# SwiGLU's input projection as seven products of quarters instead of eight, with the sums on GpSimd

## The chip, the cores and the metric

The kernel runs on one core of one Trainium2 chip. The metric is the device time of one execution in microseconds (us); lower is better. Of a kernel that is compared, several runs are made and the median is given.

The engines are TensorE (PE, matmuls; PEld is its weight load), VectorE (DVE), ScalarE (ACT), GpSimd (POOL) and SyncE (SP, which here issues the loads). Each has a queue of its own that is worked off in order; the Tile framework puts the instructions into the queues and adds semaphores.

## The reference

A trunk of two layers over 512 tokens of width 1024. Each layer has a mixer (a causal convolution group beside gated linear attention, with one output projection), a cross-attention into 256 memory tokens, and a SwiGLU block, each with a residual and a layer norm. What the change touches is the first product of SwiGLU:

```python
def swiglu(x, w_in, w_out):
    g, u = jnp.split(x @ w_in, 2, axis=-1)
    return (jax.nn.silu(g) * u) @ w_out

    # in the layer
    h = layer_norm(DEEPNORM_ALPHA * h + xa, ln2_g[l], ln2_b[l])
    ff = swiglu(h, w_ffn_in[l], w_ffn_out[l])
```

`w_in` is 1024 x 5632, the two halves of its columns being g and u (2816 each); `w_out` is 2816 x 1024. All is float32.

## The kernel before

**Products in three passes.** TensorE multiplies in a shorter float format (fp32r). Each operand is therefore split into a high part (`hi`, a copy by ACT that rounds) and a low part (`lo = src - hi`, a subtraction by DVE, or by POOL for some weights): `split`, L93 to L95. A product is three matmuls, hi·hi, hi·lo and lo·hi (`mm3`, L129 to L132), summed in a bank of PSUM. There are eight banks: four with the tag acc, two tr, two cv.

**Weights.** A chunk of 512 KB (128 partitions x 1024) is loaded by SP into one of three `stage` buffers (`raw`), split by ACT and DVE into a buffer of `ring` (four) and used (`wchunk`, L114). Which engine does the low part is set by `wlo_engines`; from the cross-attention on it is DVE for all.

**Layer norm.** `out_proj` (L244) adds the residual for each tile of 128 tokens (`tt`) and calls `layer_norm` (L168): statistics on DVE, a chain of small DVE operations for 1/sqrt (`rstd_of`), two passes over the tile with scale and bias (L177 and L183), then eight transposes on PE into two banks (`lt_ln`, L191), each bank copied to hi by ACT and to lo by DVE (L194). The transposed result hT is the moving operand of the next product, 512 tokens wide.

**SwiGLU** (L697 to L727). The 2816 columns are done in pairs of 256 columns (j = 0, 2, ... 20: eleven pairs a layer). For each pair the product has g's 256 columns and u's 256 columns: four chunks of weights, in four banks, 96 matmuls of 512 tokens. The pair j = 0 is done in two halves of 256 tokens, so that it can begin before the last tiles of the layer norm are there. Then ACT takes silu of g from PSUM, DVE multiplies by u from PSUM (L712), and the product is split into ph and pl. The pairs come in three parts (four, four and three pairs), and behind each part an output projection (`out_proj`, `po_fo`) adds its share to h. The first part's first pair stands right behind the layer norm called LN2.

**Order.** The framework's scheduler places the instructions; operations under `tc.high_priority` (the evacuation of the banks, the norms) go ahead of others. Buffers are taken from pools, and a transfer or an operation that fills a buffer waits for the last reader of what was in it.

Of the kernel before, what the change touches and what calls it, by code (L numbers as in the profile page):

```python
# [20 lines left out]
P = 128  # L21
# [18 lines left out]
RING = 4  # L40
HP = 1500
# [6 lines left out]
def trunk(ctx: ExitStack, tc, a, out):  # L48
# [26 lines left out]
    # keep s <= c in both 64-blocks [s, c]  # L75
# [10 lines left out]
    attT = const.tile([P, 2, 4, P], F32, name="attT")  # L86
    DVE.memset(attT, 0.0)
# [4 lines left out]
    # ------------------------------------------------------------ helpers  # L92
# [21 lines left out]
    def wchunk(src, nk, ncol, name, resident=False):  # L114
        """src: dram [nk*128, ncol] -> (hi, lo) views [128, nk, ncol]."""
# [52 lines left out]
    def layer_norm(tt, st, gb, name, hT=None, store=None):  # L168
# [11 lines left out]
        for i in range(2):  # L180
# [11 lines left out]
            pv = pt.rearrange("p (k t) -> p k t", k=4)  # L192
            ts_ = slice(tt * P, (tt + 1) * P)
# [50 lines left out]
    def out_proj(w, stat, name, scale, norm=None, fin=False):  # L244
        """h[tt] = scale*h[tt] + stat^T w, t-tile after t-tile; stat: list of (hi, lo) [128, T]."""
# [25 lines left out]
    # ------------------------------------------------------------ memory of the cross-attention  # L271
# [31 lines left out]
    # ------------------------------------------------------------ input norm  # L303
# [50 lines left out]
    for l in range(L):  # L354
        n_ = lambda s: f"{s}_{l}"
        w_in = a["w_in"][l]
        # -------------------------------------------------- per-layer constants
# [35 lines left out]
        def conv_taps(half):  # L393
            cts = range(half * 2, half * 2 + 2)
            cv = {ct: bank(n_(f"cv{ct}"), tag="cv") for ct in cts}
            with tc.high_priority(offset=-100000):
# [7 lines left out]
                for ct in cts:  # L404
                    ACT.activation(acc[:, ct, :], cv[ct], AF.Copy)
# [71 lines left out]
        # -------------------------------------------------- GLA state updates  # L477
# [25 lines left out]
        # -------------------------------------------------- conv norm and activation  # L503
# [3 lines left out]
        def conv_norm():  # L507
            for g in range(2):
# [4 lines left out]
                for i in range(2):  # L513
# [3 lines left out]
                    for ct in range(4):  # L517
                        PE.transpose(pt[:, ct * P:(ct + 1) * P], acc[:, ct, tt * P:(tt + 1) * P], ident)
# [6 lines left out]
                for i in range(2):  # L525
                    tt = g * 2 + i
                    ACT.activation(acc[:, :, tt * P:(tt + 1) * P], pts[i].rearrange("p (c f) -> p c f", c=4),
                                   AF.Identity, scale=y2[:, i:i + 1], bias=b2[:, i:i + 1])
# [220 lines left out]
```

## Time and profile before

| | us |
|---|---|
| runs: median (lowest to highest) | 1457.99 (1457.73 to 1458.32) |
| the profiled execution's span | 1456.5 |
| PE busy | 1427.5 (98%) |
| DVE busy | 843.2 (58%) |
| ACT busy | 489.4 (34%) |
| POOL busy | 180.5 (12%) |

The span is that of the one execution that the profiler took, the runs are timed from outside: the median lies 1.5 us above it. The profile's page gives busy times, 40 slices of the span and the chain of work that ended last. The trace behind it is asked in views: groups of instructions of one form (with busy time, mean ns of one and the idle time before them), the timeline (start in us, length in us, engine, line, operation, output<-inputs, and how many in a row are put together), and windows (the busy time of each engine in a stretch). Where instructions of one kind stand back to back, a length read from the timeline of several is shorter than the mean of one, since their ends overlap.

### The profile page before, as it was taken

The numbers are of one execution on the slowest core, as the hardware profiler recorded it, in microseconds if no ns is written. First come the engines' busy times: TensorE is split into PE (matmuls) and PEld (weight loads), VectorE is DVE, ScalarE is ACT, GpSimd is POOL, SyncE is SP. The second block draws the span as 40 slices with busy tenths as digits, with TensorE's granted clock in tenths as the row PEclk, the third lists the DMA queues.
The fourth block names the chain that finished last, engine by engine and source line by source line (L and its number), as shares of the span: only waits on it lengthen the run. The fifth ranks groups of instructions, "written<-read, shape, count | busy, mean of one in ns | idle before, by whom it ended". The sixth has DMA issues, their size and how long they took to land.

```text
span 1456.5 us, 18479 instructions
## 1 busy us (share of the span) xinstructions
PE 1427.5 (98%) x7503; PEld 1209.9 (83%) x7503; DVE 843.2 (58%) x1423; ACT 489.4 (34%) x720; POOL 180.5 (12%) x82
## 2 busy tenths in 40 slices
PE   8999999999999999999989999999999999999997
PEld 7777878988988888888888878899889888888886
DVE  6699878557433233333769996675583333342347
ACT  5553452441322123123235335324423222330330
POOL 3576220000000000000143422200000000000000
PEclk9999999999999999999999999999999999999999
DMA  6424241221333232232252323512312332331431
GB/s 230 139 73 131 86 175 59 88 76 48 123 101 116 73 101 91 83 116 94 68 156 79 100 76 129 175 59 88 116 57 90 101 101 87 101 111 49 131 116 58
DMA packets 102953, 147.43 MB, mean 101 GB/s; under 512 B 6844, under 2 KB 81296, under 8 KB 102868
## 3 DMA queue, kind: packets, MB, share of 16 engines
q1 hardware_dynamic: 102548, 145.98, 30.7%
q8 instruction: 59, 0.97, 0.3%
q10 hardware_dynamic: 320, 0.27, 0.1%
q14 instruction: 26, 0.21, 0.0%
HBM read 144.13 MB, written 2.10 MB: 100 GB/s over the span
## 4 chain that ended last, share of the span: by engine, by line
PE 81%; DVE 15%; ACT 2%; issue 1%; DMA 0%; POOL 0%; SPq 0%; DVEq 0%; ACTq 0%; POOLq 0%
PE pp_f L130 11%; PE pp_f L132 11%; PE pp_f L131 11%; DVE cv L403 8%; PE po_fo L130 5%; PE po_fo L132 5%; PE po_fo L131 5%; PE pp_xq L131 2%; PE pp_xq L130 2%; PE pp_xq L132 2%; PE po_mo L130 2%; PE po_mo L132 2%; PE po_xo L132 2%; PE po_mo L131 2%; PE po_xo L130 2%; PE po_xo L131 2%
## 5 line engine op out<-in xcount | busy, mean ns | idle before, releaser
L131 PE MATMUL pp_f<-hT_ln,w_f 128*128 128x512 f32 (+1 forms) x768 | 285.1, 372 | 0.0
L130 PE MATMUL pp_f<-hT_ln,w_f 128*128 128x512 f32 (+1 forms) x768 | 284.4, 372 | 0.0
L132 PE MATMUL pp_f<-hT_ln,w_f 128*128 128x512 f32 (+1 forms) x768 | 283.8, 371 | 0.0
L95 DVE TENSOR_TENSOR w_f<-raw_f,w_f 128x1024 fp32r<-128x1024 f32 x88 | 106.8, 1225 | 196.4 <-ACT w_f L94 196.4
L94 ACT ACTIVATE w_f<-raw_f 128x1024 fp32r<-128x1024 f32 x88 | 91.9, 1057 | 282.0 <-PE po_fo L132 125.9
L131 PEld LDWEIGHTS pp_f<-hT_ln,w_f 128*128 128x128 f32 x768 | 144.7, 188 | 24.9
L132 PEld LDWEIGHTS pp_f<-hT_ln,w_f 128*128 128x128 f32 x768 | 144.5, 188 | 25.0
L130 PEld LDWEIGHTS pp_f<-hT_ln,w_f 128*128 128x128 f32 x768 | 144.2, 188 | 24.9
L403 DVE SCALAR_TENSOR_TENSOR cv<-u,chan,cv 128x511 f32<-128x511 f32 (+28 forms) x240 | 158.8, 732 | 0.3
L131 PE MATMUL po_fo<-w_fo,ph 128*128 128x512 f32 (+1 forms) x358 | 138.2, 386 | 0.0
L132 PE MATMUL po_fo<-w_fo,pl 128*128 128x512 f32 (+1 forms) x358 | 137.8, 385 | 0.0
L130 PE MATMUL po_fo<-w_fo,ph 128*128 128x512 f32 (+1 forms) x358 | 135.7, 385 | 0.0
L95 POOL TENSOR_TENSOR w_c<-raw_c,w_c 128x1024 fp32r<-128x1024 f32 x16 | 39.1, 2458 | 552.4 <-ACT w_c L94 552.4
L263 DVE SCALAR_TENSOR_TENSOR h<-h,po_fo 128x512 f32<-128x512 f32 (+1 forms) x49 | 32.8, 675 | 118.0 <-PE po_fo L132 117.5
L95 DVE TENSOR_TENSOR w_fo<-raw_fo,w_fo 128x1024 fp32r<-128x1024 f32 x44 | 53.0, 1222 | 82.5 <-ACT w_fo L94 82.5
L94 ACT ACTIVATE hT_ln<-lt_ln 128x512 fp32r<-128x512 f32 x40 | 22.7, 596 | 169.7 <-PE lt_ln L191 169.4
L130 PEld LDWEIGHTS po_fo<-w_fo,ph 128*128 128x128 f32 x358 | 67.2, 188 | 13.5
L131 PEld LDWEIGHTS po_fo<-w_fo,ph 128*128 128x128 f32 x358 | 67.2, 188 | 13.4
L132 PEld LDWEIGHTS po_fo<-w_fo,pl 128*128 128x128 f32 x358 | 67.3, 188 | 13.4
L94 ACT ACTIVATE w_fo<-raw_fo 128x1024 fp32r<-128x1024 f32 x44 | 45.4, 1054 | 61.0 <-PE pp_f L132 23.0
L131 PE MATMUL pp_xq<-hT_ln,w_xq 128*128 128x256 f32 (+1 forms) x192 | 61.2, 321 | 0.0
L132 PE MATMUL pp_xq<-hT_ln,w_xq 128*128 128x256 f32 (+1 forms) x192 | 60.7, 319 | 0.0
(252 smaller groups left out, 2840.8 us busy)
## 6 DMA issues: line engine op xcount, KB each, us to landing
raw_f<-w_ffn_in SPq DMA_DIRECT2D x88, 512.0 KB
raw_fo<-w_ffn_out SPq DMA_DIRECT2D x44, 512.0 KB
raw_xk<-w_xkv SPq DMA_DIRECT2D x16, 512.0 KB
raw_c<-w_in SPq DMA_DIRECT2D x16, 512.0 KB
raw_xv<-w_xkv SPq DMA_DIRECT2D x16, 512.0 KB
raw_mo<-w_mix_out SPq DMA_DIRECT2D x16, 512.0 KB
raw_xq<-w_xq SPq DMA_DIRECT2D x16, 512.0 KB
raw_xo<-w_xo SPq DMA_DIRECT2D x16, 512.0 KB
```

Of the source, the lines that this page charges most:

```text
L94: ACT.activation(hi, src, AF.Copy)
L95: eng.tensor_sub(lo, src, f(hi))
L130: PE.matmul(o, lh, rh, start=start, stop=False)
L131: PE.matmul(o, lh, rl, start=False, stop=False)
L132: PE.matmul(o, ll, rh, start=False, stop=stop)
L263: DVE.scalar_tensor_tensor(h[tt][:, c0:c1], h[tt][:, c0:c1], scale, bks[c][:, :c1 - c0], ALU.mult, ALU.add)
L403: DVE.scalar_tensor_tensor(cv[ct][:, s:], u[:, ct, :T - s], wj, cv[ct][:, s:], ALU.mult, ALU.add)
```

## The change

Let g's and u's columns of a pair (256 of each) and the 1024 rows of the weight be cut so that the weight is 2 x 2 quarters: r11 and r12 are g's columns with the upper and lower 512 rows, r21 and r22 are u's. The activations are cut in the same way: rows of 512 and tokens of 256. A product of 2 x 2 quarters takes eight products of quarters, or seven with sums before and after them (one level of Strassen's method, in Winograd's form). For the pairs j = 2 to 20 the change takes the seven.

- **Sums of activations, once a layer.** The class `Quads` takes the place of hT for LN2. Besides hi and lo (`B`), ACT copies each transposed bank as it is to `qr`, and POOL forms four differences of 128x512 from these for each of the last two tiles (L301 to L304). `combine` splits the four results into T2, T3, T1, T4.
- **Sums of weights, for each pair.** POOL forms s1 = r21 + r22 (L360), s2 = s1 - r11 (L361), s3 = r11 - r21 (L364) and s4 = r12 - s2 (L368), each 128x1024. Seven buffers are split instead of four.
- **Seven products** of 2 x 4 x 3 = 24 matmuls of 256 tokens each, in the order P1, P6, P2, P7, P5, P4, P3. P1 and P2 sum in banks X (acc), P7 and P4 in W (acc), P6 stands in Y (cv), P5 and P3 in Z (cv).
- **Sums of results.** ACT copies X's first product to x. DVE adds u2 = Y + x (L400), uu = W + u2 (L411), + Z (L416), uu's other half = W + u2 (L420) and sg = Z + u2 (L425), each twice with 128x256 out of PSUM; ACT takes silu of both halves, DVE multiplies (L427) and the result is split.
- **j = 0** stays eight products (`swiglu_plain`).
- **Pools.** `stage` has five buffers instead of three, `tmp` four instead of three, `blk` fifteen instead of seventeen; new are `evp` (five) and `quad` (three of 128x1024, which hold s1 to s4, and in the mixer the convolution's acc in two halves and attT, which POOL now clears). With acc in halves, L527's operation of 512 columns becomes two of 256. At the start of the kernel the x tiles 2 and 3 are loaded one 512 KB chunk of weights later than before.

```diff
+        def take(self, i, tt, pv):
+            s = slice((tt % 2) * P, (tt % 2 + 1) * P)
+            b = self.b[i, tt // 2]
+            split(b[:, 0, :, s], b[:, 1, :, s], pv)
+            ACT.activation(self.raw[tt // 2][:, i, :, s], pv, AF.Copy)
+            if i == 1 and tt >= 2:
+                r11, r21 = (self.raw[0][:, x, :, s] for x in range(2))
+                r12, r22 = (self.raw[1][:, x, :, s] for x in range(2))
+                POOL.tensor_sub(r11, r12, r11)
+                POOL.tensor_sub(r12, r22, r12)
+                POOL.tensor_sub(r22, r22, r11)
+                POOL.tensor_sub(r21, r21, r22)
...
+    def swiglu_seven(w, q, j, ph, pl, i0, name):
...
+        w1 = split_quarter(r11, n("a11"))
+        POOL.tensor_add(s1, r21, r22)
+        POOL.tensor_sub(s2, s1, r11)
+        w6 = split_quarter(s2, n("s2"))
+        w2 = split_quarter(r12, n("a12"))
+        POOL.tensor_sub(s3, r11, r21)
+        w7 = split_quarter(s3, n("s3"))
+        w5 = split_quarter(s1, n("s1"))
+        w4 = split_quarter(r22, n("a22"))
+        POOL.tensor_sub(s2, r12, s2)
+        w3 = split_quarter(s2, n("s4"))
...
+        X = banks_of("fx", "acc")
+        product(w1, q.b[0, 0], X, True, False)
...
+        Y = banks_of("fy", "cv")
+        product(w6, t2, Y, True, True)
+        with tc.high_priority(offset=HP):
+            u2 = two(evp, 256, "e", "u2")
+            for m in range(2):
+                DVE.tensor_add(u2[m], Y[m][:, lo], x[m])
+        product(w2, q.b[1, 0], X, False, True)
...
+        Z = banks_of("fz", "cv")
+        product(w5, t1, Z, True, False)
+        with tc.high_priority(offset=HP):
+            for m in range(2):
+                DVE.tensor_add(uu[m][:, hi], Z[m][:, lo], uu[m][:, hi])
+        product(w4, t4, W, False, True)
...
+        product(w3, q.b[1, 1], Z, False, True)
+        out = []
+        with tc.high_priority(offset=HP):
+            for m in range(2):
+                DVE.tensor_add(sg[m][:, hi], Z[m][:, lo], u2[m])
+                ACT.activation(sg[m][:, hi], sg[m][:, hi], AF.Silu)
+                DVE.tensor_mul(sg[m], sg[m], uu[m])
+                split(ph[:, i0 + m, :], pl[:, i0 + m, :], sg[m])
...
-                proj_feat(w_fi, mov, [(j * P, 256, ev_fg), (DFF + j * P, 256, ev_fu)], n_(f"f{j}"), halves=j == 0)
+                if j == 0:
+                    pT += swiglu_plain(w_fi, quads, j, ph, pl, f"{l}")
+                else:
+                    pT += swiglu_seven(w_fi, quads, j, ph, pl, (j - j0) % 4, f"{l}")
```

Line numbers of the changed kernel differ from those before; the low part of `split` is L95 before and L102 after.

How the queues stand, first DVE in the middle of part 1 of layer 0 before the change: w_f are the lo parts of the next pair's four chunks (000, 001, 010, 011), sg and pl the evacuation of the pair at hand.

```order
L95 TENSOR_TENSOR w_f_000_4616<-raw_f_000_4614,w_f_000_4616 128x1024
L95 TENSOR_TENSOR w_f_001_4621<-raw_f_001_4619,w_f_001_4621 128x1024
L95 TENSOR_TENSOR w_f_010_4628<-raw_f_010_4626,w_f_010_4628 128x1024
L712 TENSOR_TENSOR sg_0_4556<-sg_0_4556,pp_f_010_4506 128x512
L95 TENSOR_TENSOR pl_0_4483<-sg_0_4556,ph_0_4482 128x512
L712 TENSOR_TENSOR sg_0_4558<-sg_0_4558,pp_f_011_4507 128x512
L95 TENSOR_TENSOR w_f_011_4633<-raw_f_011_4631,w_f_011_4633 128x1024
L95 TENSOR_TENSOR pl_0_4483<-sg_0_4558,ph_0_4482 128x512
```

And in the changed kernel, DVE in the second half of a pair there: w_s are lo parts of POOL's sums, w_a of raw quarters; fw, fz and fy are the banks W, Z and Y. The names ending in 5096 to 5111 belong to the next pair.

```order
L411 TENSOR_TENSOR uu_0_4991<-fw_0_4965,u_0_4933 128x256
L102 TENSOR_TENSOR w_s_0_4874<-s_0_4850,w_s_0_4874 128x1024
L411 TENSOR_TENSOR uu_0_4992<-fw_0_4966,u_0_4934 128x256
L102 TENSOR_TENSOR w_a_0_5096<-raw_a_0_5085,w_a_0_5096 128x1024
L416 TENSOR_TENSOR uu_0_4991<-fz_0_4995,uu_0_4991 128x256
L416 TENSOR_TENSOR uu_0_4992<-fz_0_4996,uu_0_4992 128x256
L102 TENSOR_TENSOR w_s_0_5101<-s_0_5094,w_s_0_5101 128x1024
L420 TENSOR_TENSOR uu_0_4991<-fw_0_4965,u_0_4933 128x256
L420 TENSOR_TENSOR uu_0_4992<-fw_0_4966,u_0_4934 128x256
L102 TENSOR_TENSOR w_a_0_5104<-raw_a_0_5091,w_a_0_5104 128x1024
L425 TENSOR_TENSOR sg_0_4961<-fz_0_4995,u_0_4933 128x256
L102 TENSOR_TENSOR w_s_0_5108<-s_0_5095,w_s_0_5108 128x1024
```

Additions out of PSUM stand in turn with lo parts: w3's (4874), then w1's (5096), w6's (5101), w2's (5104) and w7's (5108) of the next pair.

POOL before the change, from the mixer's output projection of layer 0 on; w_c are weights of layer 1's mixer:

```order
L95 TENSOR_TENSOR w_mo_1903<-raw_mo_1901,w_mo_1903 128x1024
L95 TENSOR_TENSOR w_mo_1913<-raw_mo_1911,w_mo_1913 128x1024
L95 TENSOR_TENSOR w_mo_1923<-raw_mo_1921,w_mo_1923 128x1024
L95 TENSOR_TENSOR w_mo_1933<-raw_mo_1931,w_mo_1933 128x1024
L95 TENSOR_TENSOR w_c_100_5742<-raw_c_100_5740,w_c_100_5742 128x1024
```

And after, from the last of these rows of the mixer on: s are the sums of the pair j = 2 (s2 and s4 are both in the buffer 3630), qr the raw quarters of LN2.

```order
L102 TENSOR_TENSOR w_mo_1944<-raw_mo_1942,w_mo_1944 128x1024
L360 TENSOR_TENSOR s_0_3629<-raw_a_0_3623,raw_a_0_3625 128x1024
L301 TENSOR_TENSOR qr_ln_0_2975<-qr_ln_0_2976,qr_ln_0_2975 128x4x128
L361 TENSOR_TENSOR s_0_3630<-s_0_3629,raw_a_0_3621 128x1024
L364 TENSOR_TENSOR s_0_3631<-raw_a_0_3621,raw_a_0_3623 128x1024
L302 TENSOR_TENSOR qr_ln_0_2976<-qr_ln_0_2976 128x4x128
L303 TENSOR_TENSOR qr_ln_0_2976<-qr_ln_0_2976,qr_ln_0_2975 128x4x128
L301 TENSOR_TENSOR qr_ln_0_2975<-qr_ln_0_2976,qr_ln_0_2975 128x4x128
L304 TENSOR_TENSOR qr_ln_0_2975<-qr_ln_0_2975,qr_ln_0_2976 128x4x128
L302 TENSOR_TENSOR qr_ln_0_2976<-qr_ln_0_2976 128x4x128
L303 TENSOR_TENSOR qr_ln_0_2976<-qr_ln_0_2976,qr_ln_0_2975 128x4x128
L304 TENSOR_TENSOR qr_ln_0_2975<-qr_ln_0_2975,qr_ln_0_2976 128x4x128
```

POOL had nothing between the mixer's output projection and the next layer's mixer; now it has twelve operations ahead of and around the first pair, and four for each pair behind it.

More of the change, by code (lines that the diff above doesn't have):

```diff
@@ L40 @@
 RING = 4
+NBLK = 15
+RAW = 5
+TMP = 4
+EVB = 5
 HP = 1500
@@ new lines, in load_quarter, with split_quarter @@
+    def load_quarter(w, kh, c0, name):
+        raw = stage.tile([P, 1024], F32, tag="raw", name=f"raw_{name}")
+        nc.sync.dma_start(raw.rearrange("p (k c) -> p k c", k=4),
+                          w[kh * 512:(kh + 1) * 512, c0:c0 + 256].rearrange("(k p) c -> p k c", p=P))
+        return raw
+    def split_quarter(raw, name):
+        w = ring.tile([P, 2, 4, 256], F32R, tag="w", name=f"w_{name}")
+        flat = w.rearrange("p j k c -> p j (k c)")
+        split(flat[:, 0], flat[:, 1], raw)
+        return w
@@ new lines, in swiglu_plain @@
+    def swiglu_plain(w, q, j, ph, pl, name):
+        ws = [[split_quarter(load_quarter(w, kh, c0, f"g{c0}{kh}_{name}"), f"g{c0}{kh}_{name}") for kh in range(2)]
+              for c0 in (j * P, DFF + j * P)]
+        banks = [[bank(f"pp_f{j}{g}{m}_{name}") for m in range(2)] for g in range(2)]
+        for t in range(2):
+            for g in range(2):
+                for kh in range(2):
+                    for m in range(2):
+                        ms = slice(m * P, (m + 1) * P)
+                        for k in range(4):
+                            mm3(banks[g][m][:, t * 256:(t + 1) * 256], ws[g][kh][:, 0, k, ms], ws[g][kh][:, 1, k, ms],
+                                q.b[kh, t][:, 0, k, :], q.b[kh, t][:, 1, k, :],
+                                kh == 0 and k == 0, kh == 1 and k == 3)
+        out = []
+        with tc.high_priority(offset=HP):
+            for m in range(2):
+                sg = tmp.tile([P, T], F32, tag="t", name=f"sg{j}{m}_{name}")
+                ACT.activation(sg, banks[0][m], AF.Silu)
+                DVE.tensor_mul(sg, sg, banks[1][m])
+                split(ph[:, m, :], pl[:, m, :], sg)
+                out.append((ph[:, m, :], pl[:, m, :]))
+        return out
@@ L375, in trunk @@
         u = block([P, 4, T], F32, n_("u"))
-        acc = lay.tile([P, 4, T], F32, tag="acc", name=n_("acc"))
+        accs = [quarter([P, 2, T], n_(f"acc{i}")) for i in range(2)]
+        attT = quarter([P, 2, 4, P], n_("attT"))
+        POOL.memset(attT, 0.0)
         qk = block([P, 2, 2, T], F32, n_("qk"))
```

99 lines of the change are left out of this document (77 added, 22 removed).

## The prediction

> **What bounds the kernel now.** First the page's busy table, its slices and the chain that ended last.
>
> ```profile
> span 1456.5 us, 18479 instructions
> ...
> PE 1427.5 (98%) x7503; PEld 1209.9 (83%) x7503; DVE 843.2 (58%) x1423; ACT 489.4 (34%) x720; POOL 180.5 (12%) x82
> ...
> POOL 3576220000000000000143422200000000000000
> ...
> GB/s 230 139 73 131 86 175 59 88 76 48 123 101 116 73 101 91 83 116 94 68 156 79 100 76 129 175 59 88 116 57 90 101 101 87 101 111 49 131 116 58
> ...
> PE pp_f L130 11%; PE pp_f L132 11%; PE pp_f L131 11%; DVE cv L403 8%; PE po_fo L130 5%; PE po_fo L132 5%; PE po_fo L131 5%; PE pp_xq L131 2%; PE pp_xq L130 2%; PE pp_xq L132 2%; PE po_mo L130 2%; PE po_mo L132 2%; PE po_xo L132 2%; PE po_mo L131 2%; PE po_xo L130 2%; PE po_xo L131 2%
> ```
>
> TensorE is busy for 98% of the span, and a third of the last chain is pp_f, the product that the change rewrites. POOL shows zeros in the stretches where SwiGLU runs. The windows view of the two SwiGLU stretches (core's time, then busy PE, PEld, DVE, ACT, POOL, granted clock, DMA share, GB/s) says it more exactly; its third row is a stretch of the mixer, used below.
>
> ```profile
> 390.00:720.00 330.00, 330.00 (x1459) 273.23 (x1459) 123.78 (x154) 83.04 (x99) 0.00 (x0) 1.00 0.30 97
> 1086.00:1440.00 354.00, 354.00 (x1660) 297.26 (x1659) 137.03 (x176) 93.46 (x112) 0.00 (x0) 1.00 0.30 98
> 100.00:110.00 10.00, 9.18 (x43) 7.00 (x42) 10.00 (x17) 1.06 (x1) 10.00 (x5) 1.00 0.25 63
> ```
>
> PE has no idle time there, the granted clock is 1.00, DVE is at 38%, ACT at 26%, POOL does nothing and the DMA engines are at 0.30. So SwiGLU is bound by TensorE's pace, and what it saves is time only as long as nothing else becomes later than PE.
>
> **What PE saves.** From the timeline of PE, the first and the last row of two stretches of matmuls, with 100 steps between the first two and 60 between the others:
>
> ```profile
> 399.33 0.39 PE L131 MATMUL pp_f<-hT_ln,w_f 128*128 128x512 f32 x1
> ...
> 422.00 0.39 PE L132 MATMUL pp_f<-hT_ln,w_f 128*128 128x512 f32 x1
> ```
>
> ```profile
> 366.70 0.28 PE L131 MATMUL pp_f<-hT_ln,w_f 128*128 128x256 f32 x1
> ...
> 373.90 0.28 PE L132 MATMUL pp_f<-hT_ln,w_f 128*128 128x256 f32 x1
> ```
>
> A matmul of 512 columns starts 22.67/100 = 0.2267 us after the one before, one of 256 columns 7.20/60 = 0.1200 us. Halving the width doesn't halve the step: 0.1067 us are per 256 columns, 0.0133 us per instruction. A pair is 4 chunks x 8 products x 3 passes = 96 matmuls of 512 now, 21.76 us; seven products of 2 x 4 x 3 = 24 matmuls of 256 are 168, 20.16 us. The eighth that is saved (2.56 us) shrinks by 72 further instructions x 0.0133 = 0.96 us. PE saves 1.60 us a pair, 16.0 us for the ten pairs of a layer, 32.0 us in all. The Trainium skill ("TensorE: Matmul & The Clock Gate", Back-to-back issue gap) gives a gap of N/2.4 + 2.5 ns for a warm single matmul; 109.2 and 215.8 ns by it would make an estimated 2.37 us a pair. The trace has 10.8 ns more at both widths, and its steps are used.
>
> **What VectorE and GpSimd get.** By form, with the mean ns behind the busy time:
>
> ```profile
> L95 DVE TENSOR_TENSOR w_f<-raw_f,w_f 128x1024 fp32r<-128x1024 f32 x88 | 106.8, 1225 | 196.4 <-ACT w_f L94 196.4
> L712 DVE TENSOR_TENSOR sg<-sg,pp_f 128x512 f32<-128x512 f32 x44 | 30.1, 687 | 15.4 <-PE pp_f L132 15.4
> L95 DVE TENSOR_TENSOR pl<-sg,ph 128x512 fp32r<-128x512 f32 x44 | 30.1, 688 | 14.0 <-ACT ph L94 14.0
> L95 DVE TENSOR_TENSOR KT<-pp_xk,KT 128x256 fp32r<-128x256 f32 x16 | 6.5, 416 | 1.3 <-ACT KT L94 1.2
> L95 POOL TENSOR_TENSOR w_v<-raw_v,w_v 128x1024 fp32r<-128x1024 f32 x8 | 19.1, 2409 | 8.6 <-ACT w_v L94 8.5
> L527 ACT ACTIVATE acc<-cvt,b,y_cln 128x512 f32<-128x512 f32 x8 | 5.8, 774 | 9.7 <-DVE b L524 9.7
> L94 ACT ACTIVATE w_f<-raw_f 128x1024 fp32r<-128x1024 f32 x88 | 91.9, 1057 | 282.0 <-PE po_fo L132 125.9 <-PE pp_f L132 98.9 <-issue 37.8
> L94 ACT ACTIVATE KT<-pp_xk 128x256 fp32r<-128x256 f32 x16 | 5.8, 378 | 8.0 <-PE pp_xk L132 8.0
> L94 ACT ACTIVATE hT_ln<-lt_ln 128x512 fp32r<-128x512 f32 x40 | 22.7, 596 | 169.7 <-PE lt_ln L191 169.4
> ```
>
> ```profile
> 360.73 3.48 DVE L95 TENSOR_TENSOR w_f<-raw_f,w_f 128x1024 fp32r<-128x1024 f32 x3
> ...
> 42.14 0.74 DVE L95 TENSOR_TENSOR KT<-pp_xk,KT 128x256 fp32r<-128x256 f32 x2
> ...
> 198.03 1.29 DVE L95 TENSOR_TENSOR cUl<-csl,cUh 128x512 fp32r<-128x512 f32 x2 [0.63 <-ACT cUh L94]
> ```
>
> Back to back a weight's lo part takes 3.48/3 = 1.16 us, an addition of 256 columns out of PSUM 0.74/2 = 0.37 us, a subtraction of 512 columns in SBUF 1.29/2 = 0.64. A pair gives DVE 7 lo parts (8.1), two products and two pl (2.6) and ten additions out of PSUM (3.7): 14.4 us, where it had 4 x 1.225 + 4 x 0.69 = 7.7. POOL gets four sums, 4 x 2.41 = 9.6 us. ACT gets seven hi parts (7.4), six copies and silus of 256 columns out of PSUM or SBUF (6 x 0.378 = 2.3) and two ph of 512 (2 x 0.596 = 1.2): 10.9 us of 20, not the bound. The weights' bytes stay the same. Alone, each engine would fit under 20.16 us.
>
> Together they don't, as the mixer's rows show (timeline):
>
> ```profile
> 199.55 2.41 POOL L95 TENSOR_TENSOR w_mo<-raw_mo,w_mo 128x1024 fp32r<-128x1024 f32 x1 [7.61 <-ACT w_mo L94]
> ...
> 200.45 2.58 DVE L95 TENSOR_TENSOR w_mo<-raw_mo,w_mo 128x1024 fp32r<-128x1024 f32 x1 [1.13 <-ACT w_mo L94]
> ...
> 202.37 2.93 POOL L95 TENSOR_TENSOR w_mo<-raw_mo,w_mo 128x1024 fp32r<-128x1024 f32 x1 [0.42 <-ACT w_mo L94]
> ```
>
> ```profile
> 44.63 5.22 POOL L95 TENSOR_TENSOR w_c<-raw_c,w_c 128x1024 fp32r<-128x1024 f32 x2 [2.96 <-ACT w_c L94]
> ...
> 45.11 5.89 DVE L95 TENSOR_TENSOR hT_ln<-xf,hT_ln 128x512 fp32r<-128x512 f32 x3 [0.77 <-ACT hT_ln L94]
> ```
>
> ```profile
> 21.48 2.37 DVE L152 SCALAR_TENSOR_TENSOR s_ln<-t_ln 128x1 f32<-128x1 f32 x1
> ...
> 104.00 0.68 DVE L463 TENSOR_TENSOR dk<-pp_qk,dk 128x512 f32<-128x512 f32 x1
> ```
>
> DVE's lo part at 200.45 should take 1.2 us; it ends at 203.03, 1.07 after POOL's end at 201.96, so it did its work when POOL was through. POOL's next one ends at 205.30, 2.27 after DVE's end. Three DVE operations and two of POOL at 44.63 alternate: 5.89 us for 3 x 0.64, and even an operation of one element per partition took 2.37. But dk, which has one operand in PSUM, took 0.68, no more than L712's product beside an idle POOL, in the stretch from 100 to 110, where POOL is busy 10.00 of 10.00. So operations of DVE on two SBUF operands and POOL's sums exclude each other, those with an operand in PSUM run beside POOL. The Trainium skill ("SBUF — State Buffer", Who interferes with whom) has it so: a DVE instruction with two SBUF inputs and a GpSimd one that reads SBUF take a lock for their whole length. It speaks against this change, which gives POOL sums in the one stage where it was empty; these rows agree with it.
>
> Between two pairs in the middle of a part the work that excludes itself is 8.1 + 2.6 + 9.6 = 20.3 us, already over 20.16. With all ten additions also outside it is 24.0. DVE's queue runs in order, so an addition gets under a sum only where its neighbours are not waiting; in the order I count four of ten (one behind w3's lo, two behind w6's, one behind w7's, which let s3, s4 and s1 go), so 24.0 - 4 x 0.37 = 22.5 us. That is the cycle I take, 2.3 us over PE's.
>
> **Where the stalls fall, per layer.** The first pair behind an output projection finds its sums made during it, and the last of a part runs with no sums of a next pair: both free. The second pair has about half the deficit left (1.2), a third one before the last all of it (2.3). Part 1 has four pairs: 1.2 + 2.3 = 3.5. Part 2 has three: 1.2. Part 0 has three and begins badly; its rows in before:
>
> ```profile
> 370.64 1.42 DVE L183 SCALAR_TENSOR_TENSOR h<-h,y_ln,gb_ln 128x512 f32<-128x512 f32 x2
> ...
> 374.86 0.60 PE L191 MATMUL lt_ln<-ident,h 128*128 128x128 f32 x4
> ...
> 388.20 0.40 PE L130 MATMUL pp_f<-hT_ln,w_f 128*128 128x512 f32 x1
> ```
>
> The last tile of LN2 is done at 372.06 and its transposes start at 374.86: 2.8 us to spare. In its chain stand nine DVE operations with two SBUF operands, and POOL now holds s1, s2, s3 (2.4 each) and three subtractions of half that size (1.2) for the stretch: 10.8 us that can alternate with the chain. I take half (5.4, as part of it falls before the chain), so PE waits 2.6 us, with bounds 0 and 8.0. Then, from the transposes' end at about 376.5 until P6 of pair 2 at 388.2 + 24 x 0.120 = 391.1, 14.6 us are there for four subtractions of POOL (4.8), s4 (2.4), the lo parts of T1 to T4 (4.6), of w1 and w6 (2.3), and the two products and lo parts of pair 0 and the tile (2.6): 16.7, so 2.1 late (0 if the cover is there, up to 7 if POOL's earlier backlog slides in). Its next pair has 2.3. Part 0: 2.6 + 2.1 + 2.3 = 7.0.
>
> **The small edits.** L527 becomes eight operations of 256 columns a layer in place of four of 512; two of 256 cost 2 x 0.378 - 0.596 = 0.16 us more than one of 512 by ACT's rows above, so 0.7 us a layer, where PE waits for the norm (0 to 1.5). x tiles 2 and 3 load one 512 KB chunk later at the start, at 230 GB/s 2.3 us; I take 0, between -2 and +2, since the weights for PE come as much sooner. Clearing attT on POOL, the deeper pools and the eight raw copies of ACT (0.6 each, beside PE's 23 us of pair 0, 192 x 0.120) are free while ACT is at 26%; without cover the copies are 4.8 us a layer, inside the bound 7 above.
>
> **Sum.** Per layer 3.5 + 1.2 + 7.0 + 0.7 = 12.4 us lost of 16.0 saved: 3.6 gained, 7.2 in both. From the profiled execution's span of 1456.5 that is 1449.3; runs are at a median of 1457.99, 1.5 above the span, so 1450.8. A measurement of this kernel can tell about 0.2% (2.9 us) from no change.
>
> **Rivals.**
> A. PE stays the bound and all is hidden: only L527 is lost, 1457.99 - 32.0 + 1.4 = 1427.4. For it: each engine alone fits. Against: the rows at 199.55 to 202.37. Chance 0.06.
> B. All ten additions run beside POOL's sums, the cycle is 20.3, 0.14 over PE, and only part 0's start is lost: 2.6 + 2.1 + 0.7 + 5 x 0.14 = 6.1 per layer, so -9.9 x 2: 1438.2. For it the dk row; against it DVE's order, where additions come in twos behind the products they wait for. Chance 0.22. The Trainium skill's "SBUF — State Buffer" (Who interferes with whom), by which a DVE instruction with at most one SBUF input does not contend with GpSimd, would allow this.
> C. Slower: DVE's and POOL's work is serial, as an addition that waits for PE holds the queue while POOL's next sum waits for a lo part behind it: cycle 24.0, 3.84 a pair over PE. Then part 1 loses 1.9 + 3.8, part 2 1.9, part 0 2.6 + (2.1 + 1.5) + 3.8, L527 0.7 and the first pairs, whose sums are late by then, 3.84 each in parts 1 and 2: 26.0 per layer of 16.0 saved, +20 in both: 1478.0. It decides from the point where the losses of a layer pass 16.0, about 23 us a pair. For it: the strict alternation at 44.63. Against: ring and staging let sums go ahead during an output projection. Chance 0.28.
>
> Forecast 0.44, its own range 1443 to 1461 (part 0 between 3 and 12). Of its 0.44, 0.27 lie below 1455.1, 0.11 within 0.2%, 0.06 above 1460.9. So faster 0.06 + 0.22 + 0.27 = 0.55, same 0.11, slower 0.06 + 0.28 = 0.34. The range from 1431 to 1481 leaves out most of A and a tail of C.
>
> **What would show it.** Right: PE's step 0.120 us in pp's place; in the windows view of SwiGLU PE with idle time, most of it ended by DVE's additions out of Y and Z; lo parts of DVE with maxima of 2.4 to 3.6 us and POOL's sums near 2.9; pairs of 22 to 23 us in the middle of part 1 and 20.2 at a part's end; a wait of the last lt_ln transposes. Wrong: sums and lo parts that overlap at their own lengths (A), a full PE after part 0 (B), the first pair after an output projection also late (C), or waits that ACT, DMA or a pool's free buffer end.

## The result, and the profile after

The changed kernel takes 1471.08 us (median of 4 runs, 1470.11 to 1472.32) against 1458.06 us (4 runs, 1457.73 to 1458.32): a ratio of 1.0088, with a 95% interval of 1.0074 to 1.0102. It is 13 us slower. The forecast was 1450.8, 7 us faster than before, with a range of its own from 1443 to 1461; the prediction's whole range went from 1431 to 1481, and the rival that ended slower was at 1478. Of the experiments below, `e3_ln2_dve` and `e10_unread_sums` had one execution each of over 3000 us; their medians include it and are 0.2 and 0.3 us lower without it.

The page of the profile after, in the lines that were shown of before:

```profile
span 1469.9 us, 22112 instructions
...
PE 1410.2 (96%) x8943; PEld 1261.8 (86%) x8943; DVE 1117.1 (76%) x1690; ACT 582.3 (40%) x892; POOL 409.1 (28%) x180
...
POOL 4476220000541243132133423300005422421510
...
PE 69%; DVE 20%; issue 8%; ACT 3%; DMA 1%; POOL 0%; SPq 0%; DVEq 0%; ACTq 0%; POOLq 0%
```

PE's busy time fell by 17 us, and the span grew by 13: PE now has 60 us without work where it had 29. The busy time fell by less than the 32 us of matmuls saved; stretches at half the clock, read below, count as busy. The chain that ended last runs through DVE for 20% of the span where it was 15%, and POOL is busy in SwiGLU. PE's waits, from the view that groups them (what waited, for whom: us in total, times, the longest):

```profile
PE fz L378 <- DVE uu L416: 10.8, 10, 1.9
PE lt_ln L198 <- DVE h L190: 10.3, 2, 5.2
PE pp_c L137 <- DVE h L273: 6.0, 1, 6.0
```

P3 waits ten times for DVE's addition out of Z, and the last tile of LN2 is late in both layers; before had no wait at either place. And PE waits once for 6.0 us in a product of the mixer, pp_c, which the change does not touch; before had a wait of 4.2 us there, shown below.

Where the time went by place: the table gives the time from the first matmul of a stage to the first of the next, as differences of starts in PE's timeline; of the stages left out none changed by more than 1.4 us. "No sums" and the others to its right are experiments that follow below.

| stage (us) | before | after | no sums | sums unread | five buffers | late sums |
|---|---|---|---|---|---|---|
| start and layer 0's pp_c | 83.86 | 85.15 | 84.69 | 86.02 | 85.73 | 84.79 |
| layer 0, mixer from r to its end | 60.09 | 61.69 | 61.70 | 61.70 | 60.09 | 61.69 |
| layer 0, first part of SwiGLU | 89.72 | 98.15 | 84.38 | 93.89 | 89.71 | 85.20 |
| layer 0, second part | 87.04 | 83.11 | 80.64 | 81.99 | 87.04 | 80.63 |
| layer 0, third part | 65.28 | 61.15 | 60.48 | 61.12 | 65.28 | 60.47 |
| layer 1, pp_c | 59.09 | 63.94 | 64.24 | 63.42 | 63.65 | 57.67 |
| layer 1, first part of SwiGLU | 89.71 | 98.78 | 84.37 | 93.77 | 89.71 | 85.13 |
| layer 1, second part | 87.04 | 83.12 | 80.63 | 81.99 | 87.04 | 80.63 |
| layer 1, third part | 65.28 | 61.14 | 60.47 | 61.13 | 65.28 | 60.47 |
| end of the last matmul | 1447.76 | 1460.07 | 1426.97 | 1449.14 | 1456.00 | 1422.11 |

The six parts of SwiGLU together are 1.4 us slower than before: the second and third parts gain 16.1, the first parts lose 17.5. The other 10.9 us of the 12.3 lie outside SwiGLU.

**The first part.** The starts of pair 0, pairs 2, 4 and 6 and the output projection, layer 0:

```profile
368.58 0.28 PE L137 MATMUL pp_f<-B_ln,w_g 128*128 128x256 f32 x1
...
399.61 0.28 PE L378 MATMUL fx<-B_ln,w_a 128*128 128x256 f32 x1
...
425.70 0.36 PE L378 MATMUL fx<-B_ln,w_a 128*128 128x256 f32 x1
...
446.57 0.28 PE L378 MATMUL fx<-B_ln,w_a 128*128 128x256 f32 x1
...
466.73 0.40 PE L137 MATMUL po_fo<-w_fo,ph 128*128 128x512 f32 x1
```

Pair 0 takes 31.0 us (24.4 before, from 363.79 to 388.20), pair 2 26.1, pair 4 20.9 and pair 6 20.16, which is PE's own time. What happens in pair 0 is read from DVE and POOL side by side. The chain of LN2's last tile on DVE, and POOL's sums:

```profile
373.59 1.71 DVE L154 SCALAR_TENSOR_TENSOR t_ln<-y_ln,v_ln 128x1 f32<-128x1 f32 x1
375.33 1.22 DVE L157 SCALAR_TENSOR_TENSOR y_ln<-t_ln,y_ln 128x1 f32<-128x1 f32 x1
376.59 2.32 DVE L154 SCALAR_TENSOR_TENSOR t_ln<-y_ln,v_ln 128x1 f32<-128x1 f32 x1
378.94 2.27 DVE L159 SCALAR_TENSOR_TENSOR s_ln<-t_ln 128x1 f32<-128x1 f32 x1
381.25 1.19 DVE L160 SCALAR_TENSOR_TENSOR y_ln<-s_ln,y_ln 128x1 f32<-128x1 f32 x1
382.47 1.83 DVE L190 SCALAR_TENSOR_TENSOR h<-h,y_ln,gb_ln 128x512 f32<-128x512 f32 x1
```

```profile
372.33 2.95 POOL L360 TENSOR_TENSOR s<-raw_a,raw_a 128x1024 f32<-128x1024 f32 x1 [164.62 <-DMA raw_a<-w_ffn_in]
375.23 1.30 POOL L301 TENSOR_TENSOR qr_ln<-qr_ln,qr_ln 128x512 f32<-128x512 f32 x1
376.48 2.41 POOL L361 TENSOR_TENSOR s<-s,raw_a 128x1024 f32<-128x1024 f32 x1
378.84 2.36 POOL L364 TENSOR_TENSOR s<-raw_a,raw_a 128x1024 f32<-128x1024 f32 x1
381.15 1.27 POOL L302 TENSOR_TENSOR qr_ln<-qr_ln 128x512 f32<-128x512 f32 x1
382.50 1.26 POOL L303 TENSOR_TENSOR qr_ln<-qr_ln,qr_ln 128x512 f32<-128x512 f32 x1
```

Each DVE operation on a 128x1 operand ends about when one of POOL's ends, and POOL's next begins then. Five operations of 0.2 us take 8.7 us. PE stands still meanwhile, and pays once more when it starts again. Its windows (busy PE second; the granted clock stands third from the end):

```profile
380.00:384.00 4.00, 0.00 (x0) 0.00 (x0) 3.93 (x3) 0.00 (x0) 3.68 (x3) 0.69 0.38 115
384.00:388.00 4.00, 3.55 (x17) 3.58 (x18) 2.17 (x4) 1.68 (x3) 0.00 (x0) 0.50 0.07 20
388.00:392.00 4.00, 4.00 (x34) 4.00 (x34) 0.18 (x1) 1.14 (x2) 3.90 (x4) 0.96 0.00 0
```

After 5.15 us without work, by the row of the transposes that ended it,

```profile
384.45 1.09 PE L198 MATMUL lt_ln<-ident,h 128*128 128x128 f32 x4 [5.15 <-DVE h L190]
```

the granted clock is 0.50 for 4 us: 17 matmuls in a window that later holds 34. So pair 0 loses 6.6 us, 5.15 of waiting and 1.5 more, which fall into the stretch at half the clock. Layer 1 has the same wait and the clock at 0.50 for longer, so its pair 0 loses 7.6, 2.4 more than the wait:

```profile
1112.00:1116.00 4.00, 3.25 (x16) 3.28 (x17) 2.18 (x4) 1.45 (x3) 0.05 (x1) 0.50 0.13 45
1116.00:1120.00 4.00, 4.00 (x25) 4.00 (x25) 0.47 (x1) 0.83 (x2) 3.69 (x3) 0.65 0.00 0
```

The Trainium skill ("TensorE: Matmul & The Clock Gate", Part 1: The HAM clock gate) has the clock fall to a half after an idle window of about 3.4 us. The trace doesn't bear out the 3.4 us, and it decides here: in windows of half a us the granted clock falls at 381.5, 2.2 us after PE's last matmul, and in layer 1 at 1112.0, 4.4 us after it.

Pair 2 loses 5.9 us. PE waits three times in it, 3.6 us together, and then runs at little over half the clock:

```profile
412.29 0.39 PE L380 MATMUL fz<-T_ln,w_s 128*128 128x256 f32 x1 [0.57 <-DVE w_s L102]
...
416.33 0.36 PE L378 MATMUL fw<-T_ln,w_a 128*128 128x256 f32 x1 [1.14 <-ACT w_s L101]
...
421.35 0.36 PE L378 MATMUL fz<-B_ln,w_s 128*128 128x256 f32 x1 [1.91 <-DVE uu L416]
```

```profile
422.00:426.00 4.00, 4.00 (x23) 4.00 (x22) 4.00 (x4) 0.00 (x0) 2.38 (x1) 0.57 0.80 261
```

In layer 1 the same three waits have the same lengths, the granted clock stays at 1.00, and the pair loses 4.5. So the clock fell once where no wait was longer than 1.91 us, and once it did not.

**A pair in the middle.** One place in the second part of layer 0, DVE and POOL together:

```profile
543.05 1.21 DVE L102 TENSOR_TENSOR w_s<-s,w_s 128x1024 fp32r<-128x1024 f32 x1
...
544.34 2.41 POOL L364 TENSOR_TENSOR s<-raw_a,raw_a 128x1024 f32<-128x1024 f32 x1 [3.56 <-DVE w_s L102]
...
544.52 3.31 DVE L102 TENSOR_TENSOR w_a<-raw_a,w_a 128x1024 fp32r<-128x1024 f32 x1
```

POOL's s3 starts when the lo part of w3 is done (it waited for the buffer), 0.18 us ahead of DVE's next lo part, which then takes 3.31 us. Over the kernel the groups say the same: lo parts of raw quarters have a mean of 2278 ns, the products sg 1124, POOL's four sums 2.4 to 2.7 us.

```profile
L102 DVE TENSOR_TENSOR w_a<-raw_a,w_a 128x1024 fp32r<-128x1024 f32 x60 | 136.7, 2278 | 17.8 <-ACT w_a L101 17.8
L102 DVE TENSOR_TENSOR w_s<-s,w_s 128x1024 fp32r<-128x1024 f32 x80 | 108.0, 1350 | 3.1 <-ACT w_s L101 3.1
...
L427 DVE TENSOR_TENSOR sg<-sg,uu 128x512 f32<-128x512 f32 x40 | 43.7, 1124 | 0.0
```

The four pairs of this part start at 510.27, 530.42, 551.26 and 573.23, and the output projection at 593.38: 20.15, 20.84, 21.97 and 20.15 us.

**Layer 1's mixer.** POOL and PE where pp_c waits:

```profile
729.60 9.32 POOL L102 TENSOR_TENSOR w_c<-raw_c,w_c 128x1024 fp32r<-128x1024 f32 x4 [46.92 <-DVE hT_ln L102]
...
732.07 2.28 DVE L154 SCALAR_TENSOR_TENSOR t_ln<-y_ln,v_ln 128x1 f32<-128x1 f32 x1
734.38 2.27 DVE L159 SCALAR_TENSOR_TENSOR s_ln<-t_ln 128x1 f32<-128x1 f32 x1
736.68 2.26 DVE L160 SCALAR_TENSOR_TENSOR y_ln<-s_ln,y_ln 128x1 f32<-128x1 f32 x1
```

It is the same alternation in a norm's chain, but no sum of the change is near. POOL makes the lo parts of four mixer weights back to back. In before they came two and two, and PE waited once for 4.2 us here:

```profile
724.44 4.71 POOL L95 TENSOR_TENSOR w_c<-raw_c,w_c 128x1024 fp32r<-128x1024 f32 x2 [519.14 <-ACT w_c L94]
...
734.34 5.19 POOL L95 TENSOR_TENSOR w_c<-raw_c,w_c 128x1024 fp32r<-128x1024 f32 x2 [5.18 <-ACT w_c L94]
```

```profile
PE lt_ln L191 <- DVE hT_ln L95: 4.2, 1, 4.2
```

Three stage buffers would have held the loads back where five don't; the run with five buffers alone, below, tests it.

### The profile page after: what moved, and what is told of

It reads as the page before. It is cut to its first block, busy times and chain, and to the rows that moved or that the text cites. A ratio compares the mean times of both kernels' runs of the same rounds, so it can differ in the third digit from the quotient of the medians.

```text
span 1469.9 us, 22112 instructions
## 1 busy us (share of the span) xinstructions
PE 1410.2 (96%) x8943; PEld 1261.8 (86%) x8943; DVE 1117.1 (76%) x1690; ACT 582.3 (40%) x892; POOL 409.1 (28%) x180
## 4 chain that ended last, share of the span: by engine, by line
PE 69%; DVE 20%; issue 8%; ACT 3%; DMA 1%; POOL 0%; SPq 0%; DVEq 0%; ACTq 0%; POOLq 0%
DVE cv L566 5%; PE po_fo L137 5%; PE po_fo L138 5%; PE po_fo L139 5%; PE pp_xq L137 2%; PE pp_xq L138 2%; PE pp_xq L139 2%; PE fz L378 2%; PE fz L380 2%; PE fz L379 2%; PE po_mo L139 2%; PE po_xo L139 2%; PE po_xo L138 2%; PE po_xo L137 2%; PE po_mo L137 2%
## 5 line engine op out<-in xcount | busy, mean ns | idle before, releaser
L360 POOL TENSOR_TENSOR s<-raw_a,raw_a 128x1024 f32<-128x1024 f32 x20 | 52.8, 2642 | 479.1 <-DMA raw_a<-w_ffn_in 436.7
L102 DVE TENSOR_TENSOR w_a<-raw_a,w_a 128x1024 fp32r<-128x1024 f32 x60 | 136.7, 2278 | 17.8 <-ACT w_a L101 17.8
L101 ACT ACTIVATE w_a<-raw_a 128x1024 fp32r<-128x1024 f32 x60 | 63.4, 1056 | 189.0 <-PE po_fo L139 128.6
L101 ACT ACTIVATE w_s<-s 128x1024 fp32r<-128x1024 f32 x80 | 84.4, 1055 | 69.4 <-PE fz L380 69.4
L102 DVE TENSOR_TENSOR w_s<-s,w_s 128x1024 fp32r<-128x1024 f32 x80 | 108.0, 1350 | 3.1 <-ACT w_s L101 3.1
L368 POOL TENSOR_TENSOR s<-raw_a,s 128x1024 f32<-128x1024 f32 x20 | 53.6, 2681 | 156.7 <-DVE w_s L102 156.7
L378 PE MATMUL fx<-B_ln,w_a 128*128 128x256 f32 x320 | 90.4, 283 | 0.0
L379 PE MATMUL fx<-B_ln,w_a 128*128 128x256 f32 x320 | 90.4, 283 | 0.0
L380 PE MATMUL fx<-B_ln,w_a 128*128 128x256 f32 x320 | 89.6, 283 | 0.0
L138 PEld LDWEIGHTS po_fo<-w_fo,ph 128*128 128x128 f32 x358 | 67.3, 188 | 13.2
L102 POOL TENSOR_TENSOR w_c<-raw_c,w_c 128x1024 fp32r<-128x1024 f32 x16 | 38.6, 2427 | 88.8 <-DVE hT_ln L102 46.9
L102 DVE TENSOR_TENSOR w_fo<-raw_fo,w_fo 128x1024 fp32r<-128x1024 f32 x44 | 53.2, 1221 | 11.3 <-ACT w_fo L101 11.3
L137 PE MATMUL pp_c<-hT_ln,w_c 128*128 128x512 f32 (+1 forms) x160 | 55.7, 357 | 6.3 <-DVE h L273 6.0
L378 PEld LDWEIGHTS fx<-B_ln,w_a 128*128 128x128 f32 x320 | 61.5, 192 | 0.2
L379 PEld LDWEIGHTS fx<-B_ln,w_a 128*128 128x128 f32 x320 | 61.5, 192 | 0.2
```

The costliest lines, as they stand in the source:

```text
L101: ACT.activation(hi, src, AF.Copy)
L102: eng.tensor_sub(lo, src, f(hi))
L137: PE.matmul(o, lh, rh, start=start, stop=False)
L138: PE.matmul(o, lh, rl, start=False, stop=False)
L360: POOL.tensor_add(s1, r21, r22)
L368: POOL.tensor_sub(s2, r12, s2)
```

## The experiments

Two theories stood at first. The one: POOL's operations and DVE's on two SBUF operands lock each other out, and this makes all the stalls. The other: DVE has too much work of its own, or the waits come from banks and buffers. A third question was what of the loss comes from the pools.

**No sums (`e1_no_sums`).** The four POOL operations in `take` are left out, and in `swiglu_seven`:

```diff
-        POOL.tensor_add(s1, r21, r22)
-        POOL.tensor_sub(s2, s1, r11)
+        s1, s2, s3 = r22, r11, r21
...
-        POOL.tensor_sub(s3, r11, r21)
...
-        POOL.tensor_sub(s2, r12, s2)
+        s2 = r12
```

> The changed kernel without any of POOL's sums: the weights' and activations' lo and hi parts are taken of the raw quarters instead of their sums, all else (seven products, additions out of PSUM, buffers) stays; the result is then another one. Theory (POOL's sums and DVE's operations on two SBUF operands lock each other out): the last tile of LN2 no longer waits, each pair takes 20.2 us and the part of the first four pairs 24.4 + 3 x 20.2 = 85 us in place of 98.2 and 98.8; the two other parts lose their 2.5 and 0.7 us of stalls; in all 33 us less than the change, 1438 us. Rival (DVE's own work of 14.4 us a pair, or the order of the banks Y and Z, makes the stalls): the stalls in the first seven-product pair and in the middle of a part stay, 1455 to 1468 us.

Measured: 1436.24 us, ratio to before 0.9852 (0.9838 to 0.9867). The first parts took 84.4 us, the others 80.6 and 60.5, PE's own time. DVE has the same operations as in the changed kernel, and POOL's sums are gone:

```profile
L102 DVE TENSOR_TENSOR w_s<-raw_a,w_s 128x1024 fp32r<-128x1024 f32 x80 | 97.5, 1219 | 21.4 <-ACT w_s L101 21.4
...
L102 DVE TENSOR_TENSOR w_a<-raw_a,w_a 128x1024 fp32r<-128x1024 f32 x60 | 73.3, 1222 | 25.3 <-ACT w_a L101 25.3
```

So DVE's own work of 14.4 us a pair, the banks and the buffers cost nothing inside SwiGLU. POOL's sums cost 34.8 us, more than the 32.0 that the product left out saves. Whether by the lock or because somebody waits for the sums, this run does not tell.

**Sums that nobody reads (`e10_unread_sums`).** POOL forms the same sums, the ones of the activations into a buffer of `quad`; the splits take the raw quarters:

```diff
-        w6 = split_quarter(s2, n("s2"))
+        w6 = split_quarter(r11, n("s2"))
...
-        w7 = split_quarter(s3, n("s3"))
+        w7 = split_quarter(r21, n("s3"))
```

(and likewise w5 from r22, w3 from r12).

> The changed kernel with all of POOL's sums formed as before, but read by nobody: the splits take the raw quarters (the result is another one). It tells the lock from the waiting for POOL's results. Theory of the lock: POOL's sums still alternate with DVE, so the chain of LN2's last tile is late by several us again, and the part of the first four pairs takes 91 to 98 us (98.2 and 98.8 with the sums read, 84.4 without sums); 1450 to 1466 us. Rival (PE and DVE waited for the sums themselves, POOL being slow): as without sums, 84 to 86 us for that part, 1436 to 1441 us.

Measured: 1460.21 us, ratio 1.0011 (1.0002 to 1.0020). The first parts took 93.9 and 93.8 us. Nothing reads the sums, and 24.0 of the 34.8 us are there again; nobody can have waited for their results. Nor did a load wait for a sum to let go of its raw quarter: the view of the loads' waits names none of the sums. DVE's lo parts of the weights take 1880 and 2090 ns on average, where they took 1219 and 1222 without sums. So these 24 us come from POOL's being busy beside DVE, which is the lock. One thing came out otherwise than expected: the last tile of LN2 was on time, as the sums waited for ACT's copies; the wait stood 13 us further on, in the first product of pair 2.

```profile
PE fx L381 <- DVE w_a L102: 9.3, 2, 4.6
```

```profile
385.28 10.66 DVE L102 TENSOR_TENSOR T_ln<-qr_ln,T_ln 128x1024 fp32r<-128x1024 f32 x4 [1.75 <-ACT T_ln L101]
395.87 3.35 DVE L102 TENSOR_TENSOR w_a<-raw_a,w_a 128x1024 fp32r<-128x1024 f32 x1
```

The four lo parts of T take 2.7 us each in turn with POOL, and w1's stands behind them. Of the other 10.9 us the runs don't say how much is waiting for the sums and how much is only that POOL's work falls elsewhere when it is read.

**All sums on DVE (`e2_dve_sums`).** All eight `POOL.` in `take` and `swiglu_seven` become `DVE.`; nothing else.

> The changed kernel with all sums of quarters on DVE instead of POOL. Theory of the lock: a sum costs DVE 1.16 us where it cost the shared port 2.4, DVE's work for a pair is 14.4 + 4 x 1.16 = 19.0 us, under PE's 20.2, and nothing alternates in the chain of LN2: the time falls to between 1438 and 1450 us. Rival (DVE's work is what is too much, and POOL takes some of it away): DVE at 94% of a pair's time stalls PE more than now, 1471 us or more.

Measured: 1447.44 us, ratio 0.9925 (0.9910 to 0.9940). The second and third parts are at PE's own time (80.6, 60.5) although DVE is busy for 18.3 us of a pair's 20.16:

```profile
520.53:540.69 20.16, 20.16 (x171) 20.16 (x170) 18.31 (x26) 10.27 (x15) 0.00 (x0) 1.00 0.35 105
```

The first parts take 87.9 and 88.6. What POOL took 2.4 us for takes DVE 1.22; on POOL it could hold up an operation of DVE for those 2.4.

**Only LN2's sums and those of pair 2 on DVE (`e3_ln2_dve`).** In `take` as above, and in `swiglu_seven`:

```diff
+        E = DVE if j == 2 else POOL
-        POOL.tensor_add(s1, r21, r22)
+        E.tensor_add(s1, r21, r22)
```

(s2, s3 and s4 likewise).

> The changed kernel with only the sums of LN2's activations and of the pair j = 2 on DVE, those of the other pairs on POOL. Theory: the alternation in the chain of LN2's last tile goes (6.6 us a layer with the slower clock behind it) and part of the 5.9 us of the pair j = 2: 8 to 12 us a layer less than the change, 1447 to 1455 us. Rival (the work at this place is too much on whichever engine it stands): the wait moves to DVE, 1464 to 1471 us.

Measured: 1460.04 us, ratio 1.0010 (1.0000 to 1.0020). The time lies between the two ranges expected. The first parts took 91.5 and 92.4 us, 6.5 less than the change, not 8 to 12; in layer 0 pair 0 took 27.4 us (31.0 in the change) and pair 2 21.9 (26.1). PE still waited 2.5 us a layer for LN2's last tile, as the sums now stood in DVE's queue ahead of its chain, and the ten waits at P3 remained (11.2 us). The place was right and the size too large.

**Five stage buffers alone (`e4_before_stage5`).** On the kernel before:

```diff
-    stage = ctx.enter_context(tc.tile_pool(name="stage", bufs=3))
+    stage = ctx.enter_context(tc.tile_pool(name="stage", bufs=5))
-    blk = ctx.enter_context(tc.tile_pool(name="blk", bufs=21 - RING))
+    blk = ctx.enter_context(tc.tile_pool(name="blk", bufs=16))
```

> The kernel before with five stage buffers instead of three (and sixteen blk buffers instead of seventeen), nothing else. Theory: at the start of layer 1 four weight chunks are staged instead of two, POOL makes their lo parts back to back (9.3 us) and alternates with the chain of the norm there: PE loses about 4.9 us at this place, and the run takes 1461 to 1464 us. Rival (that loss belongs to the new order of SwiGLU's tail or to attT): within 1.5 us of the kernel before.

Measured: 1467.00 us, ratio 1.0065 (1.0049 to 1.0082): 9 us of loss without a single changed product, more than expected. Layer 1's pp_c stage grew by 4.6, the start and layer 0's pp_c by 1.9, the xq products by 0.9 and 1.6, with differences of both signs, up to 1.6 us, elsewhere. PE's wait and POOL's four lo parts are the change's own, on a kernel whose SwiGLU is that of before:

```profile
PE pp_c L130 <- DVE h L263: 7.3, 1, 7.3
```

```profile
727.95 9.31 POOL L95 TENSOR_TENSOR w_c<-raw_c,w_c 128x1024 fp32r<-128x1024 f32 x4 [520.86 <-DVE y_ln L150]
```

**Layer 1's first lo parts on DVE, on three kernels (`e6_before_stage5_wc`, `e7_before_wc`, `e5_dve_sums_wc`).** The edit is one line; POOL then does nothing while the norm ahead of layer 1 runs:

```diff
-        wlo_engines(POOL)
+        wlo_engines(*(([DVE] * 4 if l else []) + [POOL] * 40))
```

> The kernel before with five stage buffers (1467.0 us), and the lo parts of the first four weight chunks of layer 1's mixer on DVE. Theory: the same stage falls from 63.7 to 59 us or less, the time to 1460 to 1463 us; the other 4 us of the five buffers (at the start, in the mixer's output projection and in the first xq products) stay. Rival: unchanged, 1465.5 to 1468 us.

Measured, with five stage buffers: 1461.68 us (ratio 1.0022, 1.0013 to 1.0032); pp_c of layer 1 took 56.7 us instead of 63.7, PE's wait of 7.3 fell to 1.5. So the four lo parts on POOL made this wait. The time fell by 5.3 us, not by the stage's 6.9; in the trace a later stage of the mixer grew by 1.6.

> The kernel before with three stage buffers, and only the lo parts of the first four weight chunks of layer 1's mixer on DVE. The trace of before has DVE's operations blocked for some 8 us in all at this place and PE waiting 4.2 us. Theory: the wait goes and nothing else moves, 1453 to 1456 us. Rival: DVE's queue is as late with the lo parts in it as it was with POOL's beside it, 1457 to 1459 us.

Measured, on the kernel before itself: 1453.77 us (ratio 0.9967, 0.9954 to 0.9980); the stage took 55.3 instead of 59.1. The lock had cost the old kernel about 4 us at this place.

> As the kernel with all sums on DVE (1447.4 us), and the lo parts of the first four weight chunks of layer 1's mixer on DVE instead of POOL, so that POOL does nothing while the chain of the norm in front of it runs. Theory (POOL's four lo parts in a row alternate with that chain and hold its residual, on which PE waits): the stage from layer 1's first product to its q and k product falls from 63.9 us to 59 or less, the time to 1440 to 1444 us. Rival (what waits there is ACT's four hi parts ahead of the norm's own copies, or a bank): within 1.5 us of 1447.4.

Measured, on the kernel with all sums on DVE: 1439.10 us (ratio 0.9864, 0.9849 to 0.9879), 8.3 less than without this line and a little under the range expected; the stage fell from 63.9 to 57.7.

**Four stage buffers (`e9_dve_sums_raw4`).** `RAW = 4` in the kernel with all sums on DVE.

> As the kernel with all sums on DVE (1447.4 us), with four stage buffers instead of five. Theory of the depth: at layer 1's start three chunks are staged ahead, not four, the stage there lies between 59.1 and 63.9 us, and the other places that the five buffers cost give some of it back: 1441 to 1446 us. Rival (SwiGLU needs the fifth buffer, since a pair holds four quarters): the parts of SwiGLU grow by over 1 us a layer, 1447 us or more.

Measured: 1448.72 us (ratio 0.9931, 0.9916 to 0.9946). The 1.3 us more than with five buffers lie inside the spread of the runs. The stage of layer 1 stayed at 63.6, so four buffers are as bad as five there, and SwiGLU's first parts grew by 0.4 and 0.9. The time falls into the rival's range, but not for its reason, a growth of over 1 us a layer; the theory of the depth failed.

**The halves of acc alone (`e13_before_acc_halves`).** The kernel before with two tiles for acc and with L527 in halves as in the change.

> The kernel before with only the convolution's acc in two tiles, so that the norm's four operations of 512 columns a layer become eight of 256. By the prediction 0.7 us a layer, 1.4 in all: 1459 to 1460 us. Rival: it lies beside other work in the second layer or in both, 1458 to 1458.8 us.

Measured: 1459.17 us, ratio 1.0004 (0.9995 to 1.0014), which can't be told from no change. The trace shows the mixer's end in layer 0 longer (61.73 against 60.09, as in the change) and in layer 1 shorter (79.28 against 80.60). Five buffers alone leave it at 60.09 in layer 0, so the 1.6 us there belong to the halves. The interval, -0.7 to +2.0 us, holds the prediction's 1.4 as well as nothing.

**The late sums (`e11_late_sums`).** The kernel with the sums and layer 1's first lo parts on DVE, and LN2's differences formed once, of 128x1024:

```diff
-            if i == 1 and tt >= 2:
-                r11, r21 = (self.raw[0][:, x, :, s] for x in range(2))
-                r12, r22 = (self.raw[1][:, x, :, s] for x in range(2))
+            if i == 1 and tt == 3:
+                r11, r21 = (self.raw[0][:, x] for x in range(2))
+                r12, r22 = (self.raw[1][:, x] for x in range(2))
```

> As the kernel with all sums and the first lo parts of layer 1 on DVE (1439.1 us), with the four differences of LN2's activations formed once behind the last tile (four operations of 128x1024) instead of twice, once ahead of that tile's chain. Theory: the 2.6 us of four operations leave the chain, PE's wait of 2.0 to 2.5 us a layer there falls under 0.7 and the clock no longer drops behind it: 2 to 3 us a layer, 1433 to 1436 us. Rival (they are late behind the chain, and T2 and T3 hold the first seven-product pair): 1438 to 1441 us.

Measured: 1432.95 us, ratio 0.9825 (0.9812 to 0.9838). The first parts took 85.2 and 85.1 us. The chain that took 8.7 us has its short operations, as it already had with all sums on DVE; the differences no longer stand ahead of it, and the wait at lt_ln is gone:

```profile
379.59 0.16 DVE L157 SCALAR_TENSOR_TENSOR y_ln<-t_ln,y_ln 128x1 f32<-128x1 f32 x1
379.78 0.22 DVE L154 SCALAR_TENSOR_TENSOR t_ln<-y_ln,v_ln 128x1 f32<-128x1 f32 x1
380.04 0.16 DVE L159 SCALAR_TENSOR_TENSOR s_ln<-t_ln 128x1 f32<-128x1 f32 x1
...
381.32 1.29 PE L198 MATMUL lt_ln<-ident,h 128*128 128x128 f32 x8
```

**Layer 0's first lo parts too (`e12_late_sums_wc0`).** `[DVE] * 4` for both layers.

> As the kernel with the late sums, and the first four lo parts of layer 0's mixer on DVE too. Theory: at the kernel's start POOL's lo parts also alternate with the input norm's splits (the stage from the first product to the q and k product grew by 1.4 to 3.5 us with five stage buffers): 1 to 3 us less than the kernel with the late sums. Rival (DVE has no time there, or the loads at the start set the pace): the same within 1 us, or slower.

Measured: 1431.37 us, ratio 0.9816 (0.9803 to 0.9829). The interval overlaps that of the late sums, so these 1.6 us are not settled. It is the fastest of all, 27 us under the kernel before.

## Why the prediction was wrong, point by point

- **PE's saving** was right: without sums the second and third parts take 80.6 and 60.5 us, four and three times 20.16, and the ten pairs of a layer save 16.0.
- **The lock** was right as a mechanism, and four pairs in a row behave as predicted: the first and the last of a part are free, the second loses 0.7 (predicted 1.2), the third 1.8 (2.3), a cycle of 21.97 us (22.5).
- **The first part** is where one step failed by its size: "Part 0: 2.6 + 2.1 + 2.3 = 7.0". Measured were 6.6, 5.9 and 0.7 in layer 0 and 7.6, 4.5 and 1.8 in layer 1, 13.2 and 13.9 in all. "I take half" assumed that half of POOL's 10.8 us would fall ahead of the chain. By the trace the sums waited for their loads and began at 372.33, with the chain already running, so nearly all of them alternated with it. The slow clock behind the waits (1.5 and 2.4 us in pair 0, some more in pair 2 of layer 0) stood in no term. And pair 2 was put at 2.1: with the sums of LN2 and of this pair on DVE it loses 1.8 in both layers, so the rest of its 5.9 and 4.5 comes with these sums on POOL, by the lock or by waiting for them.
- **The pools** are the step that failed outright: "Clearing attT on POOL, the deeper pools and the eight raw copies of ACT ... are free while ACT is at 26%". Five stage buffers alone cost 9.0 us. ACT was the wrong cover to look at: deeper staging lets POOL work further ahead, into the chain of a norm outside SwiGLU. The trace of before had shown that very place blocked (a wait of PE of 4.2 us, gone when the lo parts moved to DVE), and the prediction did not read it.
- **L527** was put at 1.4 us. Alone it moved the time by 0.7, which can be told neither from 1.4 nor from nothing; in layer 0 the stage grew by 1.6, not 0.7. The later load of the x tiles, put at 0, was not run alone.
- **The rivals.** 1471 lies nearer to C's 1478 than to the forecast, but C's mechanism did not occur: pairs are not serial, and the first pair behind an output projection is not late. It was the forecast's own mechanism with a first part twice as dear, and a second loss of 9 us that no case had. That 1471 lies inside the whole range at all is owed to C's 1478, so it is luck. B (1438.2) was refuted for sums on POOL.

The account closes: 1458.1 before, less 32.0 saved, plus 34.8 for POOL's sums and 9.0 for five stage buffers, is 1469.9 of the 1471.1 measured; the 1.2 left lie inside the spread of the runs. Open stay the 10.9 us by which sums that are read cost more than sums that are not, part by part, and why the xq products take 0.9 to 1.6 us longer a layer with five buffers.

## What to carry to other kernels

An idle GpSimd is not free capacity beside a VectorE that works on two SBUF operands: cost its operations as time in which VectorE may stand still, and compare with doing them on VectorE, which here was half as long. Look first at chains of tiny VectorE operations on the critical path, since each of them can cost one whole operation of GpSimd. And when a pool is deepened, ask for every user of it, far from the change too, what will now run earlier and beside what.

## What the runs showed of the hardware

Five VectorE operations of one element per partition, 0.16 to 0.22 us alone, took 1.2 to 2.3 us each, every one of them behind a different GpSimd operation: in these rows the two engines take turns, one instruction each. Two TensorE waits of 5.15 us cost 6.6 and 7.6 us, as the granted clock stayed at 0.50 for some 4 and 6 us behind them; it also fell to 0.50 once behind waits of at most 1.91 us. And TensorE kept its own pace with VectorE busy for 18.3 of a pair's 20.16 us.
